# A PEER encoder layer on one Trainium2 core: key-row split on GpSimd, a sixth gather buffer, later gathers

## The chip, the cores and the metric

The kernel runs on 1 core of one Trainium2 chip. The metric is the device time of one execution in microseconds. Engines are named as the profile names them: PE (TensorE matmul), PEld (its weight load), DVE (VectorE), ACT (ScalarE), POOL (GpSimd), SP (SyncE, which here only issues transfers).

## The reference

One encoder layer is applied to 1024 prompt frames and to 8 requests of 16 frames each, 1152 frames in 9 tiles of 128. Two attention branches come first; their outputs are merged into the residual stream. Then comes the PEER block, on which the change bears, and a per-layer embedding:

```python
q = (xi @ w_q).reshape(t, PEER_HEADS, 2, PEER_DK // 2)
s = jnp.einsum('thpc,hpnc->thpn', q, sub_keys).astype(jnp.float32)
top_s, top_i = lax.top_k(s, PEER_TOPK)
...
best_s, pos = lax.top_k(cand_s, PEER_TOPK)
idx = jnp.take_along_axis(cand_i, pos, axis=-1)
g = jax.nn.softmax(best_s, axis=-1)
hid = jax.nn.gelu(jnp.einsum('thkd,td->thk', u[idx], xi).astype(jnp.float32))
wgt = (g * hid).astype(xi.dtype)
return jnp.einsum('thk,thkd->td', wgt, v[idx])
...
gate = jax.nn.sigmoid(rms_norm(h, g_ple) @ w_ple_gate)
return h + gate * (p_l @ w_ple_proj)
```

Each frame chooses 128 experts (8 heads, 16 each) out of 128 x 128; an expert is one row of `u` (its key) and one row of `v` (its value), 1024 numbers each.

## The kernel before

The nine tiles are worked in two groups: A = tiles 8, 0, 1, 2 and B = tiles 3 to 7. The stages follow each other as group 0 (A): norm, attention, merge, routing; group 1 (B): norm, attention, merge, routing; then expansion, the dense loop, and the last stage `ple_phase`, which is called the tail here. The PEER block is computed in two ways.

**Group A by gathers.** `gather_steps` (L827) yields one step per gather: an indirect DMA on POOL (L839) brings 128 rows of 4 KB, one for each frame of the tile, into one of `RING` buffers. For a key row DVE multiplies it with the frame and sums (L842, tile `u`); for a value row DVE adds it, weighted, to the tile's sum `gya` (L844, tile `v`). There are 4 tiles x 256 = 1024 gathers, in a fixed order: 128 key rows, then 128 value rows, tile by tile. When a tile is done, its sum is stored to `h2_d` (L849). A gather needs the buffer that its predecessor by `RING` places used, so POOL waits for DVE, and DVE waits for the row's landing.

**Group B densely.** `route_phase` picks the experts (DVE: `topk16`, `route_tile`). `expand_phase` (L906) turns picks and weights into a full table `G_d`: DVE compares with an iota (`oa` L939, `obb` L941), POOL or ACT scales (`ga` L945, L950), PE multiplies them (`pg` L954), ACT copies out. Then `dense_phase` (L997) runs over all 128 key columns j. `hidden` (L970) loads the keys `us` of one j (512 KB), splits them into a high part `uh` (ACT) and a low part `ul` (L968), and makes 48 matmuls `hd` (L985) for the 640 frames. `weights` multiplies with the table and splits into `wh`, `wl`; `values` loads and splits the value rows into `vh`, `vl`; `down` (L1036 to L1038) makes, for four j at a time (`GR`) and each of five tiles, 24 matmuls into one PSUM bank `py`, which DVE adds to `yacc` (L1039, 160 times). For 36 of the 128 j, `PRE`, the hidden values are computed ahead in `hidden_phase` (L990), as filler for PE during the routing of group B, with the low part on POOL, and put in `ge_d`. The other 92 are computed in the loop, with the low part on DVE.

**The tail.** `ple_phase` (L860) takes all nine tiles: square and sum (ACT L881), normalise (DVE L883), 8 transposes (PE L224), high and low parts (`aTgl`, `aTl`, DVE L230), then for each of two column halves 24 matmuls a tile (`zp`, L207 to L209), tanh, two DVE operations (L901, L902) and the store.

**What sets the order.** The program is written stage by stage, but each engine's queue is ordered by a scheduler that plays the program on a modelled clock and takes the ready instruction of highest priority. An engine runs its queue strictly in that order. Gathers have the lowest priority (`LOW`), so they stand where the model saw an engine idle. `G0` gathers are offered after group A is routed, that is to group 1's attention, merge and routing; then `G1` or `G2` at each j of the dense loop, each batch not before the low part of that j's weights has been issued (L1019); the rest after the loop:

```python
gathers(G0)
...
gathers(G1 if j in PRE else G2, split(wh, wl, ge, nc.vector))
...
gathers(9999)
```

## Time and profile before

| | |
|---|---|
| median of 3 runs | 3841.66 us (3836.6 to 3846.74) |
| the profiled execution | 3840.13 us |
| its span, first to last instruction | 3838.4 us |
| mean granted clock of PE | 0.97 |
| busy: PE, DVE, ACT, POOL | 93%, 77%, 39%, 50% of the span |
| moved by DMA | 1010.78 MB, 263 GB/s on average |

The span is the part of an execution between the first and the last instruction; 1.7 us lie around it. The stages on the span's clock, as their instructions stand in the trace: group 0 up to 787 us, its routing and the start of group 1 to 867, group 1's attention (with gathers) to 1359, its merge to 1646, routing of group B to 1941, expansion to 2199, dense loop to 3716, tail to 3838.4. The busy time of PE is modelled and includes the pipeline, so a full PE is read from its waits beside its busy share.

### The profile page before, as it was taken

The numbers are of one execution on the slowest core, as the hardware profiler recorded it, in microseconds if no ns is written. First come the engines' busy times: TensorE is split into PE (matmuls) and PEld (weight loads), VectorE is DVE, ScalarE is ACT, GpSimd is POOL, SyncE is SP. The second block draws the span as 40 slices with busy tenths as digits, with TensorE's granted clock in tenths as the row PEclk, the third lists the DMA queues.
The fourth block names the chain that finished last, engine by engine and source line by source line (L and its number), as shares of the span: only waits on it lengthen the run. The fifth ranks groups of instructions, "written<-read, shape, count | busy, mean of one in ns | idle before, by whom it ended". The sixth has DMA issues, their size and how long they took to land.

```text
span 3838.4 us, 57414 instructions
## 1 busy us (share of the span) xinstructions
PE 3567.8 (93%) x20520; PEld 2973.3 (77%) x20520; DVE 2960.1 (77%) x5610; ACT 1486.4 (39%) x3388; POOL 1912.0 (50%) x1436
## 2 busy tenths in 40 slices
PE   7989899878889899899899899999999999999999
PEld 6656567656666566699898788889998899899977
DVE  6132112899988877799989789989999998999973
ACT  6555512446667521232468722222222222222222
POOL 5122022038777756563366455656655566655620
PEclk9999899889999999899999999999999999999999
DMA  7887723328888999983345599999999999999963
GB/s 211 256 258 234 230 88 120 106 62 283 293 303 295 315 331 329 354 292 123 107 161 226 223 317 334 321 344 327 344 338 332 330 351 337 345 325 335 339 209 106
DMA packets 416560, 1010.78 MB, mean 263 GB/s; under 512 B 39105, under 2 KB 168337, under 8 KB 413841
## 3 DMA queue, kind: packets, MB, share of 16 engines
q0 software_dynamic: 147456, 536.94, 39.4%
q1 hardware_dynamic: 239008, 405.89, 32.1%
q10 hardware_dynamic: 29808, 64.28, 4.4%
q8 instruction: 162, 2.65, 0.3%
q14 instruction: 126, 1.02, 0.1%
HBM read 920.73 MB, written 86.22 MB: 262 GB/s over the span
## 4 chain that ended last, share of the span: by engine, by line
PE 53%; DVE 18%; issue 12%; DMA 8%; POOL 6%; ACT 3%; SPq 0%; ACTq 0%; POOLq 0%; DVEq 0%
PE hd L985 14%; PE py L1036 6%; PE py L1037 6%; PE py L1038 6%; POOL v L839 3%; DMA u<-in_pu,gi 3%; DVE u L842 2%; PE Sd L552 2%; DMA v<-in_pv,gi 2%; POOL u L839 2%; PE pu L664 1%; PE pg L954 1%; DVE oa L939 1%; DVE obb L941 1%; PE z L207 1%
## 5 line engine op out<-in xcount | busy, mean ns | idle before, releaser
L839 POOL DMA_INDIRECT v<-in_pv,gi x512 | 694.4, 1356 | 502.4 <-DVE gya L844 375.8
L839 POOL DMA_INDIRECT u<-in_pu,gi x512 | 695.6, 1359 | 399.8 <-DVE u L842 263.6
L844 DVE SCALAR_TENSOR_TENSOR gya<-v,hid,gya 128x1024 f32<-128x1024 f32 x512 | 663.1, 1295 | 41.3 <-DMA v<-in_pv,gi 33.4
L842 DVE SCALAR_TENSOR_TENSOR u<-u,gn 128x1024 f32<-128x1024 f32 x512 | 625.9, 1239 | 80.3 <-DMA u<-in_pu,gi 74.4
L1036 PE MATMUL py<-vh,wh 128*128 128x512 f32 x1280 | 498.0, 391 | 6.6 <-ACT vh L967 3.4
L1037 PE MATMUL py<-vl,wh 128*128 128x512 f32 x1280 | 497.7, 390 | 0.0
L985 PE MATMUL hd<-aTh,uh 128*128 128x320 f32 x2048 | 483.1, 313 | 11.1 <-ACT gp L988 9.0
L1038 PE MATMUL py<-vh,wl 128*128 128x512 f32 x1280 | 492.1, 390 | 1.1 <-DVE wl L968 1.1
L985 PE MATMUL hd<-aTh,ul 128*128 128x320 f32 x2048 | 482.5, 313 | 5.1 <-POOL ul L968 5.0
L985 PE MATMUL hd<-aTl,uh 128*128 128x320 f32 x2048 | 482.5, 313 | 0.0
L985 PEld LDWEIGHTS hd<-aTh,uh 128*128 128x128 f32 x2048 | 350.7, 190 | 20.0 <-ACT gp L988 10.6
L985 PEld LDWEIGHTS hd<-aTh,ul 128*128 128x128 f32 x2048 | 349.5, 190 | 10.8 <-POOL ul L968 6.6
L985 PEld LDWEIGHTS hd<-aTl,uh 128*128 128x128 f32 x2048 | 350.3, 190 | 4.2
L1036 PEld LDWEIGHTS py<-vh,wh 128*128 128x128 f32 x1280 | 240.2, 188 | 52.7 <-ACT vh L967 3.9
L1038 PEld LDWEIGHTS py<-vh,wl 128*128 128x128 f32 x1280 | 240.3, 188 | 51.0 <-DVE wl L968 1.5
L967 ACT CAST uh<-us 128x1024 fp32r<-128x1024 f32 x128 | 134.4, 1050 | 367.2 <-PE hd L985 346.6
L1037 PEld LDWEIGHTS py<-vl,wh 128*128 128x128 f32 x1280 | 240.6, 188 | 45.9
L967 ACT CAST vh<-vs 128x1024 fp32r<-128x1024 f32 x128 | 133.7, 1052 | 337.3 <-PE py L1038 226.3
L967 ACT CAST wh<-ge 128x640 fp32r<-128x640 f32 x128 | 92.0, 728 | 374.8 <-PE py L1037 184.8
L1039 DVE TENSOR_TENSOR yacc<-yacc,py 128x1024 f32<-128x1024 f32 x160 | 193.4, 1216 | 44.6 <-PE py L1038 44.4
L954 PE MATMUL pg<-obb,ga 128*128 128x128 f32 x1280 | 158.0, 277 | 26.2 <-ACT ga L950 10.7
L945 POOL TENSOR_TENSOR ga<-oa,gT 128x512 f32<-128x512 bf16 x80 | 134.8, 1705 | 88.6 <-PE pg L954 55.5
(1054 smaller groups left out, 7373.5 us busy)
## 6 DMA issues: line engine op xcount, KB each, us to landing
us<-in_uT SPq DMA_DIRECT2D x128, 512.0 KB
vs<-in_pv SPq DMA_DIRECT2D x128, 512.0 KB
G_d<-stage ACTq DMA_DIRECT2D x10, 4096.0 KB
gj<-G_d SPq DMA_DIRECT2D x64, 640.0 KB
kcd<-in_kA SPq DMA_DIRECT2D x128, 256.0 KB
vcd<-in_vA SPq DMA_DIRECT2D x128, 256.0 KB
ge_d<-gp ACTq DMA_DIRECT2D x36, 320.0 KB
ge<-ge_d SPq DMA_DIRECT2D x36, 320.0 KB
```

Source lines behind the costliest of these rows:

```text
L552: nc.tensor.matmul(ps[32 * b4:32 * b4 + 32, :], q3[:, 4 * s + b4, :], rhs, start=br == 1 and q < nch, stop=True)
L839: nc.gpsimd.indirect_dma_start(out=r, out_offset=None, in_=I["pu" if k < P else "pv"], in_offset=bass.IndirectOffsetOnAxis(ap=gi[:, kk:kk ...
L842: nc.vector.scalar_tensor_tensor(r, r, 1.0, n2, op0=OP.mult, op1=OP.mult, accum_out=hid[:, kk:kk + 1])
L844: nc.vector.scalar_tensor_tensor(ya, r, hid[:, kk:kk + 1], ya, op0=OP.mult, op1=OP.add)
L945: nc.gpsimd.tensor_tensor(ga[:, c, :], oa[:, b, :, :].rearrange("p i c -> p c i"), gT[:, c0 + 4 * b:c0 + 4 * b + 4].unsqueeze(2).broadcast ...
L954: nc.tensor.matmul(pg[:, c * P:(c + 1) * P], ga[:, b0 + c, :], ob[:, b0 + c, :], start=True, stop=True)
L967: nc.scalar.copy(out_h, src)
L985: nc.tensor.matmul(ps[sp][:, 0:Nw], a[:, k, :], b[:, k, sp * Nw:(sp + 1) * Nw], start=k == 0 and q == 0, stop=k == 7 and q == 2)
L1036: nc.tensor.matmul(py[:, c], wh[:, ns], vh[:, c], start=a, stop=False)
L1037: nc.tensor.matmul(py[:, c], wh[:, ns], vl[:, c], start=False, stop=False)
L1038: nc.tensor.matmul(py[:, c], wl[:, ns], vh[:, c], start=False, stop=z)
L1039: nc.vector.tensor_tensor(yacc[n], yacc[n], py, op=OP.add)
```

## The change

Seven edits. `RING` goes from 5 to 6. `G0` goes from 400 to 335, `G1` and `G2` from 5 to 6. In `route_tile` the tiles `ri` and `e` become views of `cs`. In `expand_phase` the two comparisons `oa` of one step become one of twice the size. In `hidden` the buffers of `us` go from 3 to 2, and in the loop the low part `ul` goes from DVE to POOL. In `down` the order of the five tiles is reversed in every second group of four j, and the bank of a group's last tile is kept open for the next group's first, which is the same tile; the addition to `yacc` in between is left out (31 of 160). In `ple_phase` the five tiles of group B stand before the last tile of group A (tile 2); its pools move, the weight buffers (`whl`) go from 5 to 4, and the buffers of `h2` and `n3` from 3 to 2.

The order of three places, engine by engine, before and now (a name ends in the program's running number; `u_106` is the gather of key row 106, `v_89` that of value row 89, of one tile).

DVE at the start of group B's routing, around the memset `skbd` that opens it; `wq10l` is the low part of a query weight, `tops` the first of the top-k; before:

```order
L842 SCALAR_TENSOR_TENSOR u_106_8977,hid_8658<-u_106_8977,gn_8654 128x1024
L842 SCALAR_TENSOR_TENSOR u_107_8980,hid_8658<-u_107_8980,gn_8654 128x1024
L712 MEMSET skbd_15076 128x2048
L842 SCALAR_TENSOR_TENSOR u_108_8983,hid_8658<-u_108_8983,gn_8654 128x1024
L727 TENSOR_TENSOR wq10l<-wq10s,wq10h 128x1024
L727 TENSOR_TENSOR wq11l<-wq11s,wq11h 128x1024
L842 SCALAR_TENSOR_TENSOR u_109_8986,hid_8658<-u_109_8986,gn_8654 128x1024
L842 SCALAR_TENSOR_TENSOR u_110_8989,hid_8658<-u_110_8989,gn_8654 128x1024
L842 SCALAR_TENSOR_TENSOR u_111_8992,hid_8658<-u_111_8992,gn_8654 128x1024
L842 SCALAR_TENSOR_TENSOR u_112_8995,hid_8658<-u_112_8995,gn_8654 128x1024
L842 SCALAR_TENSOR_TENSOR u_113_8998,hid_8658<-u_113_8998,gn_8654 128x1024
```

and now:

```order
L712 MEMSET skbd_14871 128x2048
L230 TENSOR_TENSOR aTl_6582<-n2t17t_14834,aTh_6581 128x4x128
L230 TENSOR_TENSOR aTl_6582<-n2t17t_14841,aTh_6581 128x4x128
L727 TENSOR_TENSOR wq10l<-wq10s,wq10h 128x1024
L727 TENSOR_TENSOR wq11l<-wq11s,wq11h 128x1024
L727 TENSOR_TENSOR wq12l<-wq12s,wq12h 128x1024
L727 TENSOR_TENSOR wq13l<-wq13s,wq13h 128x1024
L754 MAX tops_14875<-sc_14946 128x8 x2
L754 MAX tops_14876<-sc_14960 128x8 x2
```

The gathered rows `u` that stood between the splits are gone; none stands any more from the first `wq10l` to the end of the routing, where 70 stood. By stretch, the gathered rows in DVE's order go, before to now: up to group 1's first merge addition 237 to 261; merge 93 to 74; from there to the first `wq10l` split 35 to 0; routing of group B 35 to 0; dense loop up to the last split of weights, `wl127`, 624 to 638; from there to the last addition 0 to 12; behind the last addition 0 to 39.

DVE at the end of the dense loop, the last rows `v` of tile 2, weight splits `wl` and additions to `yacc`; before:

```order
L844 SCALAR_TENSOR_TENSOR gya_28220<-v_126_33371,hid_28222,gya_28220 128x1024
L968 TENSOR_TENSOR wl_33575<-ge_33514,wh_33574 128x640
L1014 TENSOR_TENSOR ge_33586<-ge_33586,gj_33584 128x640
L844 SCALAR_TENSOR_TENSOR gya_28220<-v_127_33374,hid_28222,gya_28220 128x1024
L968 TENSOR_TENSOR wl_33647<-ge_33586,wh_33646 128x640
L1014 TENSOR_TENSOR ge_33656<-ge_33656,gj_33584 128x640
L968 TENSOR_TENSOR wl_33660<-ge_33656,wh_33659 128x640
L1039 TENSOR_TENSOR yacc_20701<-yacc_20701,py_33669 128x1024
L1039 TENSOR_TENSOR yacc_20702<-yacc_20702,py_33695 128x1024
L1039 TENSOR_TENSOR yacc_20703<-yacc_20703,py_33721 128x1024
L1039 TENSOR_TENSOR yacc_20704<-yacc_20704,py_33747 128x1024
```

and now, from the last addition on (`n38r`, `n`, `wp0l`, `aTgl` and `n3t8t` belong to the tail):

```order
L1051 TENSOR_TENSOR yacc_20406<-yacc_20406,py_33613 128x1024
L845 SCALAR_TENSOR_TENSOR gya_27889<-v_89_31683,hid_27891,gya_27889 128x1024
L845 SCALAR_TENSOR_TENSOR gya_27889<-v_90_31686,hid_27891,gya_27889 128x1024
L845 SCALAR_TENSOR_TENSOR gya_27889<-v_91_31689,hid_27891,gya_27889 128x1024
L845 SCALAR_TENSOR_TENSOR gya_27889<-v_92_31692,hid_27891,gya_27889 128x1024
L214 TENSOR_SCALAR n38r<-ss_33663 128x1
L845 SCALAR_TENSOR_TENSOR gya_27889<-v_93_31893,hid_27891,gya_27889 128x1024
L198 TENSOR_TENSOR wp0l_33860<-wp0s_33857,wp0h_33859 128x1024
L845 SCALAR_TENSOR_TENSOR gya_27889<-v_94_31896,hid_27891,gya_27889 128x1024
L885 SCALAR_TENSOR_TENSOR n_33662<-h_33660,n38r,gp 128x1024
L198 TENSOR_TENSOR wp0l_33866<-wp0s_33863,wp0h_33865 128x1024
```

The last gathered row stood ahead of the last additions; now 39 rows, `v_89` to `v_127`, stand behind the last one, among the tail's operations, and tile 2 needs the last of them.

POOL in the dense loop, its DMA issues of gathers; before:

```order
L839 DMA u_69_24298<-in_pu,gi_7765 128x1024
L839 DMA u_70_24301<-in_pu,gi_7765 128x1024
L839 DMA u_71_24304<-in_pu,gi_7765 128x1024
L839 DMA u_72_24307<-in_pu,gi_7765 128x1024
L839 DMA u_73_24510<-in_pu,gi_7765 128x1024
```

and now:

```order
L840 DMA v_115_23208<-in_pv,gi_7654 128x1024
L840 DMA v_116_23211<-in_pv,gi_7654 128x1024
L970 TENSOR_TENSOR ul_24251<-us_24248,uh_24250 128x1024
L840 DMA v_117_23214<-in_pv,gi_7654 128x1024
L840 DMA v_118_23217<-in_pv,gi_7654 128x1024
L840 DMA v_119_23292<-in_pv,gi_7654 128x1024
L840 DMA v_120_23295<-in_pv,gi_7654 128x1024
L970 TENSOR_TENSOR ul_24341<-us_24338,uh_24340 128x1024
L840 DMA v_121_23298<-in_pv,gi_7654 128x1024
L840 DMA v_122_23301<-in_pv,gi_7654 128x1024
```

The low parts `ul` of the keys stand between the gather issues; on DVE none of them is left in the loop. One more thing moves, on PE: of the `hd` matmuls of the 36 `PRE` experts, 48 an expert, 358 stood behind the expansion's first `pg`; now 736 do.

The diff, without the two lines that open it and some lines around the edits:

```diff
@@ -32,14 +32,14 @@
-RING = 5
+RING = 6
...
-G0 = 400
-G1 = 5
-G2 = 5
+G0 = 335
+G1 = 6
+G2 = 6
@@ -781,13 +781,14 @@
-        ri = rt.tile([P, 2, P], U32, tag="ri", name=f"ri{nm}")
+        flat = cs.rearrange("p h c -> p (h c)")
+        ri = flat[:, 0:256].bitcast(U32).rearrange("p (k c) -> p k c", k=2)
...
-        e = rt.tile([P, 3, P], F32, tag="e", name=f"e{nm}")
+        e = flat[:, 256:640].rearrange("p (k c) -> p k c", k=3)
         e8, e9, tt = e[:, 0, :], e[:, 1, :], e[:, 2, :]
@@ -857,12 +858,13 @@
-    def ple_phase(hp, gtiles, dtiles, yacc, aTd):
+    def ple_phase(gtiles, dtiles, yacc, aTd):
 
         st = ExitStack()
-        ga = pool(st, "pga", side="right")
+        ga = pool(st, "pga")
+        hp = pool(st, "pn", 2)
         pl = pool(st, "pl", 2)
-        wpools(st, "p", 512, 2, 5)
+        wpools(st, "p", 512, 2, 4)
         TG = len(gtiles) * P
         aTg = (ga.tile([P, 8, TG], F32R, name="aTgh"), ga.tile([P, 8, TG], F32R, name="aTgl"))
@@ -871,12 +873,12 @@
         for n, t in enumerate(gtiles):
             items.append((t, n, aTg, None))
         for n, t in enumerate(dtiles):
-            items.append((t, n, aTd, yacc[n]))
+            items.insert(-1, (t, n, aTd, yacc[n]))
         for t, n, aT, h2 in items:
             if h2 is None:
-                h2 = hp.tile([P, D], F32, tag="s", name=f"h2{t}", bufs=3)
+                h2 = hp.tile([P, D], F32, tag="s", name=f"h2{t}", bufs=2)
                 nc.sync.dma_start(h2, h2_d[t])
-            n3 = hp.tile([P, D], F32, tag="s", name=f"n3{t}", bufs=3)
+            n3 = hp.tile([P, D], F32, tag="s", name=f"n3{t}", bufs=2)
             ss = small.tile([P, 8], F32, tag="ss", name=f"ss3{t}")
             nc.scalar.activation(n3, h2, AF.Square, accum_out=ss[:, 0:1])
             r = rstd_of(ss[:, 0:1], D, 1, f"n3{t}")
@@ -935,9 +937,9 @@
                 oa = ex.tile([P, 2, P, 4], BF, tag="oa", name=f"oa{t}_{c0}")
                 ga = ex.tile([P, W, P], F32, tag="ga", name=f"ga{t}_{c0}")
                 ob = ex.tile([P, W, P], F32, tag="obb", name=f"obb{t}_{c0}")
-                for b in range(2):
-                    nc.vector.tensor_tensor(oa[:, b, :, :], iota_i,
-                                            rb[:, 0, c0 + 4 * b:c0 + 4 * b + 4].unsqueeze(1).broadcast_to([P, P, 4]), op=OP.is_equal)
+                nc.vector.tensor_tensor(oa, iota_i.unsqueeze(1).broadcast_to([P, 2, P, 4]),
+                                        rb[:, 0, cw].rearrange("p (b c) -> p b c", b=2).unsqueeze(2).broadcast_to([P, 2, P, 4]),
+                                        op=OP.is_equal)
                 nc.vector.tensor_tensor(ob, iota, rb[:, 1, cw].unsqueeze(2).broadcast_to([P, W, P]), op=OP.is_equal)
                 for b in range(2):
                     if (c0 // W) % GD == 0:
@@ -969,7 +971,7 @@
 
     def hidden(dn, ge, j, n2h, n2l, eng, pre=False):
 
-        us = dn.tile([P, D], F32, tag="s", name=f"us{j}", bufs=3).rearrange("p (k i) -> p k i", k=8)
+        us = dn.tile([P, D], F32, tag="s", name=f"us{j}", bufs=2).rearrange("p (k i) -> p k i", k=8)
         nc.sync.dma_start(us, I["uT"][j])
         uh = dn.tile([P, 8, P], F32R, tag="uh", name=f"uh{j}")
         ul = dn.tile([P, 8, P], F32R, tag="ul", name=f"ul{j}")
@@ -1009,7 +1011,7 @@
             if j in PRE:
                 nc.sync.dma_start(ge, ge_d[PRE.index(j)])
             else:
-                hidden(hp, ge, j, n2h, n2l, nc.vector)
+                hidden(hp, ge, j, n2h, n2l, nc.gpsimd)
             ge3 = ge.rearrange("p (c t) -> p c t", t=64)
             nc.vector.tensor_tensor(ge3, ge3, gj, op=OP.mult)
             wh = dn.tile([P, TD], F32R, tag="wh", name=f"wh{j}", bufs=5)
@@ -1025,18 +1027,28 @@
             split(vh, vl, vs, nc.vector)
             return vh, vl
 
+        held = [None]
+
         def down(grp, jn):
-            for n in range(len(DT)):
+
+            order = list(range(len(DT)))
+            if jn // GR % 2 == 1:
+                order.reverse()
+            for n in order:
                 ns = slice(n * P, n * P + P)
-                py = sbank(f"py{jn}{n}")
+                goes_on = n == order[-1] and jn + GR < P
+                begun = n == order[0] and jn > 0
+                py = held[0] if begun else sbank(f"py{jn}{n}")
+                held[0] = py
                 for q, (vh, vl, wh, wl) in enumerate(grp):
-                    a, z = q == 0, q == len(grp) - 1
+                    a, z = q == 0 and not begun, q == len(grp) - 1 and not goes_on
                     for hf in range(2):
                         c = slice(512 * hf, 512 * hf + 512)
                         nc.tensor.matmul(py[:, c], wh[:, ns], vh[:, c], start=a, stop=False)
                         nc.tensor.matmul(py[:, c], wh[:, ns], vl[:, c], start=False, stop=False)
                         nc.tensor.matmul(py[:, c], wl[:, ns], vh[:, c], start=False, stop=z)
-                nc.vector.tensor_tensor(yacc[n], yacc[n], py, op=OP.add)
+                if not goes_on:
+                    nc.vector.tensor_tensor(yacc[n], yacc[n], py, op=OP.add)
 
         ws = [weights(0)]
         for j in range(0, P, GR):
@@ -1103,14 +1115,14 @@
         hidden_phase(hp, *aT1)
         r2s.close()
         expand_phase()
-        dp = pool(de, "dp")
+        dp = pool(de, "dp", side="right")
         yacc = [dp.tile([P, D], F32, name=f"yacc{t}") for t in DT]
         dense_phase(hp, yacc, *aT1)
         gathers(9999)
+        hs.close()
+        ple_phase(A, DT, yacc, aT1)
+        de.close()
         sg.close()
-        ple_phase(hp, A, DT, yacc, aT1)
-        de.close()
-        hs.close()
     s1.close()
     top.close()
 
```

## Rows read from the trace of the kernel before

**Rows 1.** The table by stretch; each line: stretch, length, then the columns its first row names.

```profile
core 0: us, PE busy (x) PEld busy (x) DVE busy (x) ACT busy (x) POOL busy (x), PEclk, DMA share, GB/s
867.00:1359.00 492.00, 421.82 (x2583) 315.85 (x2584) 432.75 (x825) 315.14 (x877) 367.69 (x308) 0.95 0.88 296
1359.00:1543.00 184.00, 174.97 (x607) 112.72 (x605) 144.31 (x211) 29.92 (x38) 121.45 (x93) 0.99 0.93 342
1543.00:1646.00 103.00, 93.83 (x407) 73.71 (x408) 80.70 (x118) 29.51 (x43) 61.82 (x44) 0.89 0.95 353
1646.00:1941.00 295.00, 271.86 (x1729) 263.04 (x1728) 284.00 (x1239) 106.36 (x180) 116.12 (x65) 0.97 0.49 161
1941.00:2199.00 258.00, 231.84 (x1817) 225.29 (x1817) 228.20 (x244) 200.24 (x519) 152.07 (x87) 0.99 0.51 205
2199.00:3716.00 1517.00, 1508.88 (x8126) 1352.79 (x8124) 1371.88 (x1515) 373.51 (x530) 873.88 (x620) 1.00 0.93 328
3716.00:3838.40 122.40, 112.05 (x504) 89.82 (x504) 58.31 (x80) 37.01 (x60) 4.77 (x8) 0.96 0.41 137
```

**Rows 2.** Waits of PE (matmul) from 2300 to 3690 us: total, times, longest.

```profile
PE py L1036 <- ACT wh L967: 2.7, 1, 2.7
```

**Rows 3.** The chain of work that ended last, one piece of 108 matmuls in the loop.

```profile
3436.74 15.85 PE hd L985 x108
```

**Rows 4.** Waits of DVE (VectorE) for gathered rows, 867 to 1359 us.

```profile
DVE u L842 <- DMA u<-in_pu,gi: 15.9, 17, 2.5
DVE gya L844 <- DMA v<-in_pv,gi: 13.4, 12, 2.5
```

**Rows 5.** Groups of instructions, DVE, 1543 to 1646 us: count | busy us, mean ns.

```profile
L842 DVE SCALAR_TENSOR_TENSOR u<-u,gn 128x1024 f32<-128x1024 f32 x35 | 46.2, 1339 | 0.0
```

**Rows 6.** The same groups, DVE, 1646 to 1941 us.

```profile
L844 DVE SCALAR_TENSOR_TENSOR gya<-v,hid,gya 128x1024 f32<-128x1024 f32 x16 | 26.6, 1666 | 0.0
...
L842 DVE SCALAR_TENSOR_TENSOR u<-u,gn 128x1024 f32<-128x1024 f32 x19 | 25.0, 1332 | 0.0
```

**Rows 7.** Timeline, 1631 to 1636 us: start us, us, engine, line, operation.

```profile
1631.02 1.22 DVE L842 SCALAR_TENSOR_TENSOR u<-u,gn 128x1024 f32<-128x1024 f32 x1
...
1631.41 6.35 POOL L968 TENSOR_TENSOR ul<-us,uh 128x1024 fp32r<-128x1024 f32 x2 [0.53 <-ACT uh L967]
...
1632.16 3.38 DVE L842 SCALAR_TENSOR_TENSOR u<-u,gn 128x1024 f32<-128x1024 f32 x1
```

**Rows 8.** Groups of instructions, POOL (GpSimd), 1941 to 2199 us.

```profile
L968 POOL TENSOR_TENSOR ul<-us,uh 128x1024 fp32r<-128x1024 f32 x7 | 17.5, 2499 | 0.0
```

**Rows 9.** Groups of instructions, DVE, 2199 to 3716 us (dense loop).

```profile
L844 DVE SCALAR_TENSOR_TENSOR gya<-v,hid,gya 128x1024 f32<-128x1024 f32 x368 | 472.4, 1284 | 19.1 <-DMA v<-in_pv,gi 12.9 <-issue 1.4 <-DVE gya L844 0.7
...
L1039 DVE TENSOR_TENSOR yacc<-yacc,py 128x1024 f32<-128x1024 f32 x160 | 193.4, 1216 | 44.6 <-PE py L1038 44.4
...
L968 DVE TENSOR_TENSOR ul<-us,uh 128x1024 fp32r<-128x1024 f32 x88 | 107.4, 1221 | 2.9 <-ACT uh L967 1.9 <-PE hd L985 0.8
```

**Rows 10.** Waits of DVE, 2199 to 3690 us: total, times, longest.

```profile
DVE u L842 <- DMA u<-in_pu,gi: 29.8, 28, 2.7
...
DVE ge L1014 <- DMA ge<-ge_d: 18.9, 9, 6.0
DVE vl L968 <- ACT vh L967: 16.2, 19, 2.9
```

**Rows 11.** Groups of instructions, DVE, 3716 to 3838.4 us (tail).

```profile
L901 DVE SCALAR_TENSOR_TENSOR tgp<-tgp,pl 128x512 f32<-128x512 f32 x18 | 12.4, 690 | 42.7 <-ACT tgp L900 42.7
...
L883 DVE SCALAR_TENSOR_TENSOR n<-h,n31r,gp 128x1024 f32<-128x1024 f32 x1 | 1.3, 1285 | 0.7 <-POOL n31r L215 0.7
```

**Rows 12.** Timeline, 3728 to 3733 us: a tile is loaded, then squared.

```profile
3728.90 0.33 SPq L878 DMA_DIRECT2D h<-h_d  x1
...
3732.51 1.06 ACT L881 ACTIVATE n<-h 128x1024 f32<-128x1024 f32 x1 [1.28 <-DMA h<-h_d]
```

**Rows 13.** Instructions on one tile, zp, of the tail's second column half: first and last start.

```profile
L207 PE MATMUL zp<-wp1h,aTh x40: 392/397/400, 3804.8 to 3832.2; 128*128 128x512 f32 x40
```

## The prediction, made before the changed kernel was run

> **What bounds the kernel now.** I read the table by stretch first, since a share of the whole span hides what ends last where [rows 1]. In the dense loop PE is busy for 1508.9 of 1517 us; its waits there come to one of 2.7 us [rows 2], and the chain runs for long pieces through PE alone, 108 matmuls in 15.85 us, 147 ns each [rows 3]. So 1517 us, 40% of the span, is PE's own pace. DVE, the engine from which the change takes work in this stretch, is busy 1371.9 us there, close behind PE. Before and after the loop things stand otherwise. In group 1's attention (867 to 1359 us) PE idles for 70 of 492 us, DVE for 59, of which 29 go to gathered rows that have not landed [rows 4]. From 1543 to 1941 PE idles for 9 and 23 us, DVE for 22 and 11: both are nearly full. In the expansion (1941 to 2199) PE idles for 26 of 258 us. In the tail PE is busy 112 of 122.4.
>
> The sum is made against the profiled execution, 3840.1 us, which lies 1.5 us below the median.
>
> **Group 1's attention, where gathers are added.** DVE's order has 24 more gathered rows there. At 1.28 us each [rows 9] they come to 31 us: the upper end, if all lie on the path. The lower end is a gain of 29 us, if a sixth buffer removes every wait for a row's landing. DVE has 30 us of other idle time, but PE's 70 idle us say that PE waits on a chain through DVE too. I take +12, on the side of the added work, since the sixth buffer can only advance a row's landing and not DVE's own work. The merge behind it (1359 to 1543) loses 19 rows, 24 us; but PE is busy 175 of 184 us there with work that stays, so at most 9 us could go, and I count nothing of them, since the 24 rows ahead will have pushed gathers into it.
>
> **From there to the end of group B's routing, where they are taken away.** The order shows that all 70 rows go. In the first stretch they are 35 rows, 46.2 us of DVE [rows 5]; but PE idles for only 9 of 103 us there, and PE's work does not shrink, so at most 9 us go. In the routing 35 rows go, 26.6 + 25.0 = 51.6 us [rows 6], on a DVE that is 96% busy. PE's filler, the `PRE` experts' matmuls, can leave this stretch, and by the order it does. So nearly all of it is gained: -53, with one or two us of the hold shown at the loop. Together **-62**; the ends are -88 (the first stretch yields 35, by a chain that skips PE's filler) and -40 (nothing in the first stretch, three quarters in the routing).
>
> **Expansion.** What PE did not do earlier it does here. Behind the expansion's first matmul stand 736 - 358 = 378 more `hd` matmuls, 7.9 experts at 48 x 147 ns = 7.05 us [rows 3], 55.5 us. PE's idle 26 us can take some: 55.5 - 26 = +29. Each of these experts also brings a `ul` on POOL, 8 x 2.5 = 20 us [rows 8], which may hold DVE (below). Against it, the 160 comparisons `oa`, of 512 elements each, become 80. Two operations of 512 elements cost 2 x 690 where one of 1024 costs 1285 [rows 11], 95 ns less, so 80 x 0.095 = 8 us of DVE. DVE is not ahead of PE here, and I count 1 us of it: **+28**, with ends of -8 (PE's work hidden, `oa` gained) and +56 (no idle time usable).
>
> **Dense loop.** All five parts are DVE's or POOL's; the matmuls stay, and so does PE's 1517 us, if the others keep up. Off DVE: 92 `ul` at 1.22 us, 112 us [rows 9], and 31 additions to `yacc` at 1.216, 38 us. Onto DVE: 14 more gathered rows, 18 us. But the moved operation is not gone. The timeline shows what a POOL `ul` does to its neighbour [rows 7]: two of them lie in 1631.41 to 1637.76, and the DVE operation on a gathered row that starts beside them takes 3.38 us, where the one just before took 1.22. That is 2.16 us lost on DVE for a `ul` that cost it 1.22. If each of 92 meets such an operation, DVE loses 92 x 2.16 = 199 us. So DVE has 1372 - 112 - 38 + 18 + 199 = 1439 us of work, and with its waits for rows, tables and high parts (29.8 + 18.9 + 16.2 [rows 10], 12.9 [rows 9]) 1517 of 1517. It stands at the edge. I take **+5**, with ends of 0 (many `ul` meet an addition, which reads PSUM, or a wait) and +45: the 44.6 us for which DVE now waits for `py` at the additions [rows 9] is time that a DVE behind its work no longer can wait away.
>
> The Trainium skill (SBUF — State Buffer, "Who interferes with whom") says that the port pair that DVE shares with GpSimd is an exclusive lock, so that whoever starts second waits for the whole instruction of the other, and that a DVE operation with one SBUF input or none stands outside of it. The trace agrees nearly: a hold of 2.16 us [rows 7] for an instruction of 2.5 [rows 8]. By the letter of the rule each of the 92 would cost 0.34 us more, DVE would have 1470 us of work, and my sum would be 31 us higher. I go by the rows.
>
> **Tail.** Here is the largest loss. No gathered row stood behind the last addition; now 39 do, and tile 2, which needs all of them, is the last tile on PE in each column half. Counting DVE's order from the last addition to `v_127`: 39 x 1.284 = 50 us; eight of the nine `n` at 1.28 = 10; 32 operations of 512 elements at 0.69 = 22 [rows 11]; four weight splits at 1.22 = 5: 87 us. Then the sum of tile 2 is stored and loaded: 3.6 us from load to use [rows 12], the store as much by the same row, 7 us; then square, `n32`, transposes and splits, some 4. So tile 2's matmuls of the first half start 98 us into the tail. PE's order puts nothing of the second half ahead of them, so behind them come 24 + 216 matmuls. At (3832.2 - 3804.8) / 117 = 0.234 us [rows 13] that is 56 us; from the last matmul to the end it is some 6 us (to 3838.4). The tail takes 160 us instead of 122.4: **+37**, with ends of +25 (the tail's DVE work fits into the waits of PE) and +55 (the rows' landing, 6 in flight, paces DVE). Putting group B's tiles first hides part of this; it has 8 tiles x 24 x 0.234 = 45 us of PE work to cover 98 us.
>
> **At nothing.** `ri` and `e` as views, the buffers of `us`, `h2`, `n3` and `whl`, the reversed order and the open bank add no work; what they might delay is a load, and PE's loop shows no wait on one.
>
> Sum: 12 - 62 + 28 + 5 + 37 = +20, so 3860 for the profiled execution and **3862** as a median. Within the terms' likelier halves it lies at 3850 to 3890.
>
> **Rivals.**
> - *The gain in front comes whole, the cost behind not* (faster). The filler that leaves the routing finds room: first stretch and routing -85, expansion +20 with `oa` gained, attention -10 by the sixth buffer, loop 0, tail +30: -45, about 3797. For it: 97.8 us of DVE work go from stretches where DVE is full. Against it: PE's work moves and does not shrink, and PE idles for only 9 + 23 + 26 = 58 us there. It decides if the expansion grows by less than 20 us.
> - *The port becomes the loop's bound* (slower by more). POOL holds DVE for the whole 2.5 us and the py waits stay: 1439 + 31 + 78 + 45 = 1593 us, +76; half way between this and the edge above, +60 in place of +5: 3917. POOL then also gets its rows later. For it: DVE stands at the edge. Against it: 129 additions are not held, and POOL, with 874 of 1517 us busy, has room.
> - *Front and end cancel* (no change). Attention 0, -70, +28, 0, +37: -5, 3837. For it: every term is an exchange of places for the same 1024 rows.
> - *The change doesn't do what it says.* A split moved to POOL takes nothing off DVE if it blocks it for longer, and of the rows put later only 14 go into the loop to its last split; 51 stand behind it. My forecast counts with this already.
>
> **How the numbers follow.** My forecast has 0.40, the bound by the port 0.16 (both slower); no change 0.21; faster 0.23. The range, 3798 to 3915, leaves out the lower half of the first rival and the upper half of the second, about 2 in 10. Some 0.3%, 11.5 us, is what a measurement can tell from no change.
>
> **What would show it.** Right: the routing of B ends some 50 us earlier on its stretch, the expansion lengthens by 20 to 40, the loop stays at 1517 with two-input operations on DVE of 3 us and more beside `ul`; DVE's gathered rows fill the first 85 us of the tail while PE idles before `zp` of tile 2. Wrong: PE waits in the loop for `ul` or `wl` by tens of us (the port), an expansion that does not grow, or a tail under 140 us.

## The result, and the profile after

The changed kernel takes 3885.86 us (median of 4 runs, 3882.03 to 3889.08), the kernel before 3844.2 us in the same series: a ratio of 1.0106, 95% interval 1.009 to 1.0122. It is slower by 42 us. The forecast was 3862, slower by 20: the time lies inside the range, on the forecast side, but the gap is twice the one forecast.

The profiled execution has a span of 3880.3 us. Cut at the same landmarks in both traces (the first or last start of the instructions on one tile), the difference of 41.9 us falls on the stretches like this:

| stretch, and its end | before | after | difference | forecast |
|---|---|---|---|---|
| up to group 1's merge: first `pu` matmul | 1331.6 | 1355.7 | +24.1 | +12 |
| merge: first `wo10l` split on DVE | 211.3 | 207.3 | -4.0 | 0 |
| to the routing of B: first `wq10l` split | 103.6 | 78.0 | -25.6 | -9 |
| routing of B: first `pg` matmul | 301.2 | 246.0 | -55.2 | -53 |
| expansion: first `py` matmul | 255.2 | 275.7 | +20.5 | +28 |
| dense loop: last `py` matmul's end | 1512.9 | 1548.5 | +35.6 | +5 |
| tail | 122.6 | 169.1 | +46.5 | +37 |

The table by stretch of the changed kernel, cut at these landmarks, answers to [rows 1] (stretch, length, PE, PEld, DVE, ACT, POOL busy, granted clock, DMA share, GB/s):

```profile
867.00:1355.70 488.70, 403.22 (x2486) 306.35 (x2485) 449.50 (x908) 308.81 (x869) 377.74 (x314) 0.90 0.88 298
1355.70:1563.00 207.30, 206.01 (x696) 130.60 (x697) 134.42 (x208) 35.01 (x43) 118.85 (x84) 1.00 0.85 309
1563.00:1641.00 78.00, 73.07 (x333) 57.70 (x332) 37.41 (x49) 28.45 (x43) 7.26 (x8) 0.96 0.56 195
1641.00:1887.00 246.00, 227.97 (x1452) 221.35 (x1451) 231.52 (x1188) 97.67 (x166) 67.92 (x25) 0.97 0.28 93
1887.00:2162.70 275.70, 274.52 (x2174) 273.56 (x2173) 237.47 (x173) 211.52 (x538) 189.92 (x100) 1.00 0.58 227
2162.70:3711.20 1548.50, 1517.45 (x8114) 1353.46 (x8112) 1449.57 (x1454) 368.38 (x527) 1158.36 (x735) 0.99 0.92 328
3711.20:3880.30 169.10, 121.31 (x504) 95.94 (x504) 105.37 (x120) 39.35 (x62) 56.62 (x44) 0.85 0.64 226
```

From 1563 to 1887 DVE has no gathered row left, where 70 stood, 35 ahead of the first `wq10l` split and 35 behind it; in the expansion PE is busy 274.5 of 275.7 us. In the loop DVE is busy 1449.6 us, but PE now idles for 31 of 1548.5 us, 8 of 1517 before [rows 1]; in the tail it idles for 48 of 169.

What PE waits for in the loop (2155 to 3690 us: total, times, longest), where before there was almost nothing [rows 2]:

```profile
PE py L1047 <- ACT wh L969: 19.3, 13, 3.6
PE py L1049 <- DVE wl L970: 7.5, 8, 1.6
PE hd L987 <- POOL ul L970: 1.2, 1, 1.2
```

So `ul` itself hardly ever comes late on POOL. What DVE waits for there [rows 10]:

```profile
DVE yacc L1051 <- PE py L1049: 51.0, 39, 4.6
DVE u L843 <- DMA u<-in_pu,gi: 16.8, 16, 2.4
DVE ge L1016 <- ACT ge L990: 14.2, 14, 4.3
```

For `py` it waited less in the kernel before, over the same part of the loop (2199 to 3690 us):

```profile
DVE yacc L1039 <- PE py L1038: 29.8, 29, 2.2
```

PE waits for `wh`, the high part of the weights. That is ACT's, but ACT waits for DVE's product `ge`, twice as long as in the kernel before; before and now:

```profile
ACT wh L967 <- DVE ge L1014: 165.7, 56, 10.2
ACT wh L969 <- DVE ge L1016: 335.4, 83, 8.9
```

One wait of PE for `wh`, in the order of time, from the timelines of the four engines:

```profile
2908.73 1.05 ACT L969 CAST uh<-us 128x1024 fp32r<-128x1024 f32 x1 [4.81 <-DMA us<-in_uT]
2909.69 0.76 ACT L990 ACTIVATE ge<-hd 128x320 f32<-128x320 f32 x2
...
2909.86 2.40 POOL L970 TENSOR_TENSOR ul<-us,uh 128x1024 fp32r<-128x1024 f32 x1 [2.82 <-ACT uh L969]
...
2910.47 2.47 DVE L1016 TENSOR_TENSOR ge<-ge,gj 128x640 f32<-128x640 f32 x1 [3.05 <-ACT ge L990]
2912.87 1.27 DVE L845 SCALAR_TENSOR_TENSOR gya<-v,hid,gya 128x1024 f32<-128x1024 f32 x1
2914.06 0.81 DVE L1016 TENSOR_TENSOR ge<-ge,gj 128x640 f32<-128x640 f32 x1
...
2914.91 1.35 ACT L969 CAST wh<-ge 128x640 fp32r<-128x640 f32 x2 [4.46 <-DVE ge L1016]
...
2915.68 0.79 PE L1047 MATMUL py<-vh,wh 128*128 128x512 f32 x1 [3.24 <-ACT wh L969]
```

ACT makes `uh` and then the activation `ge`, one right after the other. The first releases POOL's `ul`, the second DVE's product. So the product starts 0.6 us behind `ul` and takes 2.47 us, where the next one, alone, takes 0.81. ACT's `wh` starts when that second product is done, which stands behind a gathered row: of PE's wait of 3.24 us the hold accounts for 1.66. In the whole loop 46 of the product's 127 instances overlap a `ul`; they take 2777 ns on average, the others 814 at the median. The view of line L1016 shows the spread (min/median/max):

```profile
L1016 DVE TENSOR_TENSOR ge<-ge,gj x127: 808/817/3739, 2166.6 to 3688.1; 128x640 f32<-128x640 f32 x127
```

Adding up, for every DVE operation that overlaps a `ul`, what it takes beyond the median of its kind alone, gives 194 us for 89 `ul`, 2.18 us each (90 on `ge`, 39 and 37 on gathered rows `u` and `v`, 19 on `wl`, 9 on `vl`). An addition to `yacc`, which reads PSUM, is not held: 1213 ns beside a `ul` (4 of them here, 14 in experiment 4), 1212 alone.

In the tail, the timelines at its start and where tile 2 comes:

```profile
3725.56 1.97 PE L224 MATMUL n3t8t<-ident,n 128*128 128x128 f32 x8 [14.36 <-DVE n L885]
...
3803.95 1.28 DVE L845 SCALAR_TENSOR_TENSOR gya<-v,hid,gya 128x1024 f32<-128x1024 f32 x1
...
3805.26 0.32 SPq L850 DMA_DIRECT2D h_d<-gya  x1
...
3808.32 0.37 SPq L880 DMA_DIRECT2D h<-h_d  x1
...
3813.26 1.06 ACT L883 ACTIVATE n<-h 128x1024 f32<-128x1024 f32 x1 [6.86 <-DMA h<-h_d]
...
3818.53 0.79 PE L207 MATMUL zp<-wp0h,aTgh 128*128 128x512 f32 x1
```

The last gathered row is added 94 us into the tail, tile 2's matmuls start at 107 us and the end comes 62 us later. PE has waited for `n` of tile 8 (14.4 us), of tile 2 (11.0) and of tile 1 (5.5).

### The profile page after: what moved, and what is told of

Same layout as the page of the kernel before. It is cut to its first block, busy times and chain, and to the rows that moved or that the text cites. A ratio compares the mean times of both kernels' runs of the same rounds, so it can differ in the third digit from the quotient of the medians.

```text
span 3880.3 us, 57361 instructions
## 1 busy us (share of the span) xinstructions
PE 3575.2 (92%) x20520; PEld 2977.0 (77%) x20520; DVE 3005.7 (77%) x5407; ACT 1482.8 (38%) x3388; POOL 2202.1 (57%) x1528
## 5 line engine op out<-in xcount | busy, mean ns | idle before, releaser
L840 POOL DMA_INDIRECT u<-in_pu,gi x512 | 723.6, 1413 | 288.9 <-DVE u L843 134.5
L840 POOL DMA_INDIRECT v<-in_pv,gi x512 | 705.3, 1377 | 290.8 <-DVE gya L845 178.3
L845 DVE SCALAR_TENSOR_TENSOR gya<-v,hid,gya 128x1024 f32<-128x1024 f32 x512 | 692.3, 1352 | 14.7 <-DMA v<-in_pv,gi 8.8
L843 DVE SCALAR_TENSOR_TENSOR u<-u,gn 128x1024 f32<-128x1024 f32 x512 | 657.5, 1310 | 47.0 <-DMA u<-in_pu,gi 46.4
L1047 PE MATMUL py<-vh,wh 128*128 128x512 f32 x1280 | 501.3, 394 | 21.6 <-ACT wh L969 19.3
L970 POOL TENSOR_TENSOR ul<-us,uh 128x1024 fp32r<-128x1024 f32 x128 | 346.8, 2711 | 209.6 <-ACT uh L969 201.6
L1016 DVE TENSOR_TENSOR ge<-ge,gj 128x640 f32<-128x640 f32 x128 | 193.4, 1520 | 38.8 <-DMA vs<-in_pv 22.5
L1051 DVE TENSOR_TENSOR yacc<-yacc,py 128x1024 f32<-128x1024 f32 x129 | 155.3, 1214 | 51.6 <-PE py L1049 51.4
```

The lines of the kernel that those rows point to most:

```text
L840: nc.gpsimd.indirect_dma_start(out=r, out_offset=None, in_=I["pu" if k < P else "pv"], in_offset=bass.IndirectOffsetOnAxis(ap=gi[:, kk:kk ...
L843: nc.vector.scalar_tensor_tensor(r, r, 1.0, n2, op0=OP.mult, op1=OP.mult, accum_out=hid[:, kk:kk + 1])
L845: nc.vector.scalar_tensor_tensor(ya, r, hid[:, kk:kk + 1], ya, op0=OP.mult, op1=OP.add)
L970: return eng.tensor_tensor(out_l, src, out_h.bitcast(F32), op=OP.subtract)
L1016: nc.vector.tensor_tensor(ge3, ge3, gj, op=OP.mult)
L1047: nc.tensor.matmul(py[:, c], wh[:, ns], vh[:, c], start=a, stop=False)
```

## The experiments

Each ratio is to the kernel before on the same chip, with its 95% interval. Stretches are those of the table above.

**1. `ul` back on DVE.**

```diff
-                hidden(hp, ge, j, n2h, n2l, nc.gpsimd)
+                hidden(hp, ge, j, n2h, n2l, nc.vector)
```

> The changed kernel with the key rows' low part `ul` in the loop back on DVE, all else as changed. Theory (the port): each POOL `ul` holds a DVE operation with two SBUF inputs for about 2 us, DVE falls behind its order, its `ge` and `wl` come late and PE waits at the seam from `hd` to `py`. Then the loop from first to last `py` matmul falls from 1548.5 us to 1512 to 1522, PE's gaps at that seam go, and the time is about 3886 - 33 = 3853 us (3845 to 3862). Rival (the loop's new form: open bank, two `us` buffers, 14 more rows): the loop stays at 1540 to 1555 us and the time at 3880 to 3895, because DVE even has 112 us of `ul` more.

Measured: 3839.97 us, 0.9981 (0.9967 to 0.9995). The loop takes 1509.8 us; the other stretches are those of the changed kernel within some 2 us. The table by stretch for this loop, PE's waits in it, and DVE's longest:

```profile
2162.20:3672.00 1509.80, 1504.43 (x8113) 1350.12 (x8111) 1357.82 (x1545) 368.53 (x527) 928.87 (x645) 1.00 0.94 336
```

```profile
PE hd L987 <- ACT ge L990: 4.5, 1, 4.5
PE py L1047 <- DVE yacc L1051: 0.7, 1, 0.7
DVE yacc L1051 <- PE py L1049: 89.3, 71, 3.3
```

DVE does 91 operations more and is busy 92 us less. The move of `ul` costs 38.7 us of loop, the whole of it, and with `ul` on DVE everything else in the loop's new form costs nothing. Of the 38.7 us PE is idle for 25.7 (31.1 against 5.4); by the other 13.0 its busy time is longer, for the same matmuls.

**2. The move alone, in the kernel before.**

```diff
-                hidden(hp, ge, j, n2h, n2l, nc.vector)
+                hidden(hp, ge, j, n2h, n2l, nc.gpsimd)
```

> The kernel before with one edit alone: `ul` in the loop on POOL. Theory (the port): the loop of 1513 us grows by 25 to 60 us, since here no addition is saved and DVE has 1372 - 112 + about 190 = 1450 us of work and the old waits; everything ahead of the loop and the tail stay; about 3844 + 40 = 3884 us. Rival (the loop's new form): the loop grows by less than 10 us, the time is 3836 to 3854.

Measured: 3903.28 us, 1.0142 (1.0115 to 1.0169). The loop grows from 1512.9 to 1565.6 us, by 52.7; the rest stays within 5. The holds add up to 187 us for 87 `ul`, again none on an addition. So the move is bad by itself and not through its company; this kernel has three buffers for `us`, so having only two is not the cause either.

**3. `ul` on POOL in every second group of four j.**

```diff
-                hidden(hp, ge, j, n2h, n2l, nc.gpsimd)
+                hidden(hp, ge, j, n2h, n2l, nc.gpsimd if j // GR % 2 else nc.vector)
```

> The changed kernel with the loop's `ul` on POOL only in every second group of four j, on DVE in the others: 46 on each. Theory A (each group stands for itself: a held `ge` makes PE wait at that group's seam, and DVE cannot make it good later): about half of the 38 us between the changed kernel's loop and that with `ul` on DVE, so a loop of 1525 to 1535 us, 3886 - 19 = 3867. Theory B (DVE's throughput over the whole loop decides; with 46 holds it has 1410 us of work, well under 1517): a loop of 1508 to 1518 us, about 3848.

Measured: 3848.81 us, 1.0005 (0.9997 to 1.0014); loop 1515.6 us. With 47 `ul` on POOL the holds are 96.5 us, half, but the loop loses 6 us against experiment 1, not 19. This fits theory B, by which DVE makes up in one group what it lost in the other: with 1402.2 us of work it still has 113.4 us of waits. There is an edge, as forecast, and the changed kernel lies beyond it.

**4. All 160 additions, `ul` on POOL.**

```diff
-                goes_on = n == order[-1] and jn + GR < P
-                begun = n == order[0] and jn > 0
+                goes_on = False
+                begun = False
```

> The changed kernel (`ul` on POOL) with all 160 additions: the bank is not held over from one group to the next. Theory (with `ul` on POOL, DVE sets the loop, so work taken off or put on it counts nearly in full): 31 more additions of 1.21 us, the loop grows by 20 to 40 us, 3886 + 30 = 3916. Rival (an addition stands in DVE's wait for PE and costs nothing): loop within 8 us of 1548.5, 3878 to 3895.

Measured: 3871.9 us, 1.0066 (1.0053 to 1.0079). Both expectations miss: with 31 more additions the loop is 11 us *shorter*, 1537.6 us. DVE's own waits in it:

```profile
DVE yacc L1051 <- PE py L1049: 29.6, 28, 3.5
```

DVE is busy 28 us more (1478.0) and waits 21 us less for `py`; the holds are the same in sum (189 us), but 53 of them fall on `ge` in place of 90, and 14 `ul` meet an addition in place of 4. So an addition left out is no gain beside a POOL `ul`. The place of the holds doesn't explain it: experiment 2 has 38 us of them on `ge` and the longest loop of all, experiment 5 has 104 and a loop of 1539.3 us.

**5. The gathers dealt as before, all else changed.**

```diff
-G0 = 335
-G1 = 6
-G2 = 6
+G0 = 400
+G1 = 5
+G2 = 5
```

> The changed kernel with the gathers dealt as before (400, 5, 5), sixth buffer and all else as changed. In its order 261 rows stand ahead of the first merge addition as in the changed kernel, 97 in the merge, 37 and 5 up to the expansion, none behind the last addition. Theory (the deal makes B's gain and the tail's loss, the sixth buffer the longer attention): attention still 24 us longer than before, the routing of B some 45 shorter, expansion 15 to 20 longer, loop 25 to 35 longer, tail 122 to 130 us: about 3844 + 25 = 3869 us (3855 to 3880). Rival for the tail (the new order of the tiles lengthens it): the tail stays above 145 us.

Measured: 3865.43 us, 1.0042 (1.0028 to 1.0057). Attention 25 us longer than before, routing 40 shorter, expansion 10 longer, loop 26 longer, tail 125.2 us. With no row left behind the loop the tail is nearly that of before: the rows make its length, not the new order of tiles. The attention is as long as with 335 rows offered.

**6. and 7. `ul` on DVE, and 370 or 380 offered.** Experiment 1 with one edit:

```diff
-G0 = 335
+G0 = 370
```

> The changed kernel with `ul` on DVE in the loop and 370 gathers offered to group 1 in place of 335, six at each j: by its order 261 and 97 rows stand up to the end of group 1's merge, 12 up to the routing, 636 and 13 in the loop, 5 behind it. Theory: the routing and the expansion stay as in the changed kernel, the stretch before the routing gives some 10 us back, the loop takes 1510 us as in the run with `ul` on DVE, and the tail, where PE idled for tile 2, falls from 169 us to about 130: 3840 + 12 - 39 = 3813 us (3800 to 3825), faster than the kernel before by some 0.8%. Rival (the tail's length comes from the new order of the tiles or from the loads, not from the rows behind the loop): tail above 150 us, 3835 or more.

> As the run before with 380 offered to group 1: 22 rows between merge and routing, 641 and 3 in the loop, none behind it. Theory: ten rows more cost up to 10 us ahead of the routing, the eight fewer at the end give 5 to 10 back: the same within 8 us, 3805 to 3825. Rival (the loop cannot take five rows more): the loop grows beyond 1520 us and the time beyond 3830.

Measured: 3826.35 us, 0.9949 (0.9936 to 0.9962), and 3821.54 us, 0.9941 (0.9928 to 0.9954). Loops of 1511.5 and 1512.9 us, tails of 130.6 and 127.1. The first came 13 us above what was expected, since the merge took 10 us more with 97 rows than with 74 and the routing 4. Both are faster than the kernel before.

**8. The second column half ahead of tile 2.** The changed kernel, with

```diff
-        for cg in range(2):
+        parts = [(0, items[:-1]), (1, items), (0, items[-1:])]
+        for k, (cg, part) in enumerate(parts):
...
-            for t, n, aT, h2 in items:
+            for t, n, aT, h2 in part:
```

> The changed kernel, with the tail's matmuls of the second column half put ahead of tile 2's first half: eight tiles first half, nine tiles second half, then the first half's weights loaded again for tile 2. Theory (in the tail PE stands idle for tile 2 because DVE has 39 rows to add, and nothing of the second half may pass): tile 2 still begins about 105 to 115 us into the tail, but only 48 matmuls stand behind it, so the tail falls from 169 us to 125 to 138: about 3886 - 38 = 3848 us. Rival (rows land too late, or DVE has the second half's work too and so delays the rows): tile 2 begins 20 us or more later and the tail stays at 150 us or more, 3867 or above.

Measured: 3873.85 us, 1.0066 (1.0042 to 1.009); tail 159.2 us, only 10 less. Tile 2's `n` is there about as early as expected (its transposes start 114 us into the tail), but PE has little time to fill ahead of it: the first half of the other eight tiles does not take the 45 us of its matmuls, it lasts until 94 us into the tail. Each tile's `n` and `aTl` stand between gathered rows in DVE's order, and DVE is nearly full (38.6 of 40 us from 3760 to 3800). PE's clock is also lower there, 0.75 granted from 3725 to 3760 us; the two shares were not told apart. From there PE has the second half to do in any case, 216 matmuls and tile 2's 24. So the rows delay more than the last tile.

**9. The tail's tiles in the old order.** The kernel of experiment 7, with

```diff
-            items.insert(-1, (t, n, aTd, yacc[n]))
+            items.append((t, n, aTd, yacc[n]))
```

> The same fastest kernel, with the tail's tiles in the order of the kernel before (8, 0, 1, 2, then group B). No row is left behind the loop there. Theory: with no rows left the order of the tiles is nearly free; tail 120 to 127 us instead of 127, 3815 to 3822. Rival (tile 2's store and load, which then stand early, hold PE): tail 130 us or more.

Measured: 3826.66 us, 0.9946 (0.993 to 0.9962); tail 128.5 us. Neither expectation holds exactly; the new order gains nothing that can be told when no row is left (the profiled attention was 8 us longer here, with the same instructions).

**10. Five gather buffers.** The kernel of experiment 7, with

```diff
-RING = 6
+RING = 5
```

> The fastest kernel so far (`ul` on DVE in the loop, 380 gathers offered to group 1) with five gather buffers in place of six; its order has 246 rows in place of 261 ahead of the first merge addition, and 39 in place of 22 between merge and expansion. Theory (the sixth buffer is what lengthened group 1's attention: it lets 15 more rows onto a DVE whose time there is the path): the first merge matmul, at 1353.7 us, comes 12 to 18 us earlier, what follows up to the expansion gives 10 to 20 back, and the time is within 12 us of 3821. Rival (the attention is longer for another reason): the first merge matmul stays at 1350 us or later.

Measured: 3821.38 us, 0.9938 (0.9923 to 0.9952). The first merge matmul comes at 1339.4 us, 14 earlier for 15 rows fewer; the stretches behind give 19 back and the expansion takes 7 less. So the sixth buffer lengthens the attention by letting in more rows, at some 0.95 us each, and brings nothing in all. (One profile shows it; the eleven profiles with 261 rows have this matmul at 1351.6 to 1361.9 us.)

**11. All additions, `ul` on DVE.** The kernel of experiment 7 with the edit of experiment 4.

> The same fastest kernel, with all 160 additions to `yacc` (no bank held over). Theory (with `ul` on DVE the loop is at PE's pace and DVE has time left): the loop stays at 1508 to 1518 us and the time within 6 us of 3821. Rival (the 31 additions, 38 us of DVE, are what gives DVE its time): a loop beyond 1525 us, 3835 or more.

Measured: 3828.01 us, 0.9955 (0.9941 to 0.997). The loop takes 1514.6 us: at PE's pace 31 additions cost 2 us. Of the 4.6 us by which the two profiled spans differ, the other 2.8 lie in the tail (129.9).

**12. Two comparisons `oa` again.** The kernel of experiment 7, with

```diff
-                nc.vector.tensor_tensor(oa, iota_i.unsqueeze(1).broadcast_to([P, 2, P, 4]),
...
+                for b in range(2):
+                    nc.vector.tensor_tensor(oa[:, b, :, :], iota_i,
...
```

> The same fastest kernel, with the two comparisons `oa` of a step as two instructions again. Theory (the expansion is at PE's pace, which is busy 270 of 271 us there): from the first `pg` to the first `py` within 4 us of 274.8. Rival (DVE sets it, and an instruction saved counts): 6 to 12 us longer.

Measured: 3830.43 us, 0.9961 (0.9947 to 0.9975). The expansion takes 282.3 us in place of 274.8, so the rival holds: 7.5 us. With one comparison PE sets the pace there; with two DVE holds it up. The table by stretch for it, with one `oa` and with two:

```profile
1905.00:2179.80 274.80, 274.23 (x2174) 273.52 (x2173) 239.80 (x174) 212.16 (x540) 180.92 (x96) 1.00 0.58 226
```

```profile
1911.00:2193.30 282.30, 276.04 (x2174) 273.50 (x2173) 252.01 (x253) 211.88 (x542) 167.60 (x96) 1.00 0.56 220
```

and PE's waits there, with one and with two:

```profile
PE pg L956 <- DVE obb L943: 0.6, 2, 0.3
```

```profile
PE pg L956 <- DVE obb L943: 6.3, 11, 1.4
```

## Why the prediction was right or wrong

**Dense loop: +5 forecast, +35.6 measured. This is the step that failed.** The price of a `ul` was right: 2.16 us from one row [rows 7], 2.18 measured on average; 199 us in sum forecast, 194 measured. What failed is "it stands at the edge". The sum gave DVE 1439 us of work and 78 us of waits, 1517 of 1517, and left out the 44.6 us for which DVE waits for `py` [rows 9], as if DVE could use all of that time when late. Measured: 1449.6 us of work and 98.9 of waits, and they are other waits than those counted. The 78 us for rows, tables and high parts shrank to some 20; the wait for `py`, put at nothing, came to 51.0, and that for ACT's `ge` to 14.2. So the upper end, +45 with the 44.6 us left in, and the rival of the port, +60, came nearer than the forecast, but in part by luck.

How much of the waits DVE can use shows against experiment 1: its work in the loop is 91.8 us longer, its waits are 53.1 us shorter (152.0 to 98.9), and the loop grows by the other 38.7. Nor are the waits that are left a fixed amount: for `py` they are 89.3 us there and 29.6 in experiment 4, whose waits come to 59.6 in all. Experiments 1 and 2 tie the loss to `ul`, experiment 3 shows the edge; why 98.9 us of waits remain in the changed kernel is open. A smaller slip in the same term: 14 more rows were counted up to the last weight split, but 12 more stand between it and the last addition, inside the loop.

By the Trainium skill (SBUF — State Buffer, "Who interferes with whom") a DVE operation with two SBUF inputs waits for a whole GpSimd instruction that reads SBUF and that it finds under way, and one with at most a single SBUF input does not, outside the 2-port performance modes that the page excepts. The runs agree on both: holds of 2.18 us on average beside instructions of 2.6, as DVE's operation can start a little later (0.6 us in the timeline above), and none on the additions.

**Tail: +37 forecast, +46.5 measured.** The mechanism was right, and most steps a little small: 94 us to the last row in place of 87 (DVE waits 3.0 us for rows, 3.6 for `wp0h`), 8 to store and load in place of 7, 5 in place of 4 to the first matmul, and 62 to the end as worked out. Experiments 5, 6 and 7 show that the tail follows the rows left behind the loop (0, 5 and 0 rows: 125, 131, 127 us). The first half of the eight other tiles did lie ahead of tile 2, but spread over 94 us and not packed into 45. Whether the new order hides any of the delay was not tested with the rows left there; with none left it gains nothing (experiment 9).

**Group 1's attention: +12 forecast, +24.1 measured.** The upper end was 31, all 24 rows on the path; that is nearly what happened. I let the sixth buffer count as help. Experiment 10 shows the opposite: it is the buffer that lets 15 of these rows in. That DVE's order has them ahead of the merge was there to be seen; that the number offered has no part in it (experiment 5 has 261 rows there too, with 400 offered) I did not ask.

**To the end of the routing: -62 forecast, -80.8 measured.** The routing was right (-53, -55.2). In the first stretch "PE's work does not shrink" was wrong: 80 of PE's instructions there were `hd` matmuls, filler for experts computed ahead; after the change 6 are left, and 24 `pp` have become 8. The end of -88, "by a chain that skips PE's filler", had this.

**Expansion: +28 forecast, +20.5 measured.** The merged `oa` was priced at 8 us and put down as hidden; experiment 12 gives 7.5, all of it on the path. With the PE part as worked out, 55.5 - 26 = +29, that makes 21.5. With two comparisons PE waits 6.3 us for DVE, with one 0.6. The Trainium skill (Perfetto Trace Analysis, "Optimizing Scalar/DVE Operations") says that larger operations help an engine that is saturated, as each has a fixed cost; the trace agrees: here that was worth 12 us of DVE, 252.0 to 239.8.

**At nothing: right in part.** With `ul` on DVE the open bank gains 2 us of loop at most (experiment 11, which keeps the reversed order), and two buffers for `us` cost the loop nothing (experiment 1). In the changed kernel the open bank costs 11 us (experiment 4), and the 38 us that the sum took off DVE for the 31 additions brought nothing.

In sum the front gained 40.2 us where 22 were forecast, and loop and tail lost 82.1 where 42 were. The two errors are of opposite sign, and that the time lies inside the range owes to this. The first two tests named in the prediction came out as stated for the forecast (a shorter routing, an expansion longer by 20), as did the operations held beside `ul` and the rows in the tail; the loop did not stay at 1517. Of the sign named for the port, waits of PE by tens of us for `ul` or `wl`, only 8.7 us came; the larger wait, 19.3 us, was for `wh`.

The change without the move of `ul`, with 380 gathers offered, is faster than both kernels: 3821.5 us, 0.9941 of before. Five buffers or six make no difference to it.

## What to carry to other kernels

Before moving an elementwise operation from VectorE to GpSimd, find one instance of each side by side in the trace and count what the neighbour loses: here 1.22 us were saved and 2.18 lost for each `ul`. When the load of an engine with a fixed order is added up against a bound, its waits are reserve only in part, and which of them stay can't be read off the trace before: here 92 us more work took 53 us out of the waits and lengthened the loop by 39. And work that is dealt to a later place by a scheduler has to be looked up where it lands: 39 rows came out behind the last addition, where the tail had to wait for them.

## What was not expected of the hardware and the schedule

- Leaving out 31 additions (38 us of DVE) beside POOL's `ul` made the loop 11 us longer than with them (experiment 4); without `ul` on POOL it made no difference beyond 2 us. Why is open.
- Half of the `ul` on POOL cost 6 us of loop, all of them 38.7: the loss is not in proportion.
- Right behind the wait of 3.2 us shown above, PE's matmuls come 0.43 us apart, where they came 0.23 us apart ahead of it. The timeline of PE there, and the table by stretch for the wait and the 4.3 us behind it:

```profile
2902.74 0.39 PE L1047 MATMUL py<-vh,wh 128*128 128x512 f32 x1
2902.97 0.39 PE L1048 MATMUL py<-vl,wh 128*128 128x512 f32 x1
...
2916.27 0.63 PE L1048 MATMUL py<-vl,wh 128*128 128x512 f32 x1
2916.70 0.63 PE L1047 MATMUL py<-vh,wh 128*128 128x512 f32 x1
```

```profile
2912.00:2915.70 3.70, 0.46 (x5) 0.20 (x3) 3.70 (x4) 0.79 (x2) 2.91 (x3) 1.00 1.00 371
2915.70:2920.00 4.30, 4.30 (x13) 3.58 (x14) 4.30 (x6) 0.56 (x1) 2.56 (x2) 0.60 0.97 307
```

The granted clock is 1.00 during the wait, in which PE is busy 0.46 of 3.7 us, then 0.60 on average: for a part of the 4.3 us it is at the lower of its two levels, 1.2 and 2.4 GHz. So a wait can cost more than its length, but few did: in the trace of the changed loop 17.0 us, in four stretches, lie at the lower level, in that of experiment 1 6.8 us. By an estimate from these, half of the difference, the clock makes 5 of the 38.7 us. Over the whole loop the granted clock falls from 1.00 to 0.99, over the tail from 0.96 to 0.85.
